# Latent attention in rounded parts, and the mixer's output projection divided along its inputs and run between the heads

## The chip, the cores and the metric

The kernel runs on one core of one Trainium2 chip. The time is device time of one launch in microseconds (us), as the median of several runs. A profile of one execution says when each instruction ran on each engine: TensorE (PE, and PEld for its weight loads), VectorE (DVE), ScalarE (ACT), GpSimd (POOL) and SyncE, whose queue (SPq) issues the DMAs.

## The reference, cut to what matters

Two transformer blocks over 256 latent tokens of width 1024. The second block has two layers and a second stream of 256 context tokens beside the latent one. Its first layer mixes tokens with a gated linear attention (GLA) and, beside it, with multi-head latent attention (four heads; 128 content and 64 rotary dimensions per key, 128 per value). Both outputs, 512 wide each, are joined, and one projection brings the 1024 inputs back to the model's width:

```python
def dense_attention(q, k, v, scale):
    s = jnp.einsum('bqhd,bkhd->bhqk', qi, k).astype(jnp.float32) * scale
    p = jax.nn.softmax(s, axis=-1).astype(v.dtype)
    return jnp.einsum('bhqk,bkhd->bqhd', p, v)
...
        yc, yl = even_mixer(hc, hl, cos, sin, even_w_in[i], ...)
        xl = post_norm(xl, g2 * yl)
        xl = post_norm(xl, 0.5 * g3 * swiglu(modulate(xl, sh3, sc3), ffn2_w_in[l], ffn2_w_out[l]))
        if not last:
            xc = post_norm(xc, cg2 * yc)
            xc = post_norm(xc, 0.5 * cg3 * swiglu(modulate(xc, csh3, csc3), ffn2_w_in[l], ffn2_w_out[l]))
```

Latent queries see all 512 keys (256 latent and 256 context), context queries the 256 context keys. All is float32.

## The kernel before

Activations lie with features on the 128 partitions and tokens along the free dimension: columns 0 to 255 are the latent stream, 256 to 511 the context. Dense products are made in rounded parts: every operand is held as a rounded high part and the remainder as a low part (type float32r), and `mm3` (line 221) makes high x high, high x low and low x high, three matmuls. `split` (line 256) makes the parts of an activation: a ScalarE copy that rounds, then a VectorE subtraction. `wunit` (line 198) does the same for a unit of weights of 128 x 1024 elements, 512 KB, behind its DMA; four staging tiles and three tiles each for high and low parts are shared by all weights of the kernel.

`even` (line 765) is the first layer's mixer. It projects, runs the GLA (`gla_core`, line 987), and then, from line 821, the part that the change touches:

- `mla` (line 917) for the context (`s=1`, two key tiles) and then for the latent stream (`s=0`, four key tiles). For each head and each of two query tiles, `weights` makes two full-precision score products (content, line 927, and rotary, line 928) into one PSUM bank `d` (four buffers), then row maximum, exponential, reciprocal and scaling (`softmax`, line 453); `finish` transposes the weights on TensorE (line 935), copies them out of PSUM (line 936), and after the second query tile `values` (line 942) makes the value products (line 945) and splits the head's output into `ym`. `push` (line 448) delays each `finish` by one step, so that the scores of one tile stand ahead of the transposes of the tile before.
- `gla_norm` (line 959) for both streams, between the two calls of `mla`, gives the linear attention's part `yg`.
- `mix_group` (line 744) is a quarter of the output projection for one stream: 256 output columns, eight input tiles (four from `yg`, four from `ym`), two weight units, 48 matmuls, and two gated additions into `res` (line 741). The context's four groups run one behind each latent head; the latent stream's four stand behind the heads.
- `after(1)` and `after(0)` are the layer norms (`post_ln`, line 342) and the modulation (line 368) of the context and of the latent stream, whose results `u` feed the next feed-forward products (`swiglu`, line 710), the context's first.

`need` (line 442) runs pieces of the conditioning's weight stream until its rows are there. Within an engine instructions run in order. That order is set at compile time by a scheduler that takes ready instructions by their place in the program, with offsets for weight splits (`AHEAD`) and for the emptying of PSUM (`EVAC`). Tile pools are stacked: the pool `mlaw` takes the memory of the GLA's closed pools, and an instruction that writes a tile waits for the last reader of what lay there.

Of the kernel before, what the change touches and what calls it, by code (L numbers as in the profile page):

```python
# [10 lines left out]
F32 = mybir.dt.float32  # L11
F32R = mybir.dt.float32r
# [6 lines left out]
P = 128  # L19
D = 1024  # L20
KD = D // P
S = 256
# [93 lines left out]
class Net:  # L116
# [28 lines left out]

    # ------------------------------------------------------------- set-up
    def setup(self):
# [48 lines left out]

    # ------------------------------------------------------------- dense pieces
    def wunit(self, w, k0, kc, c0, ncols):
# [60 lines left out]

    # ------------------------------------------------------------- token statistics  # L260
    def colsum(self, acc, n, T):
# [118 lines left out]

    # ------------------------------------------------------------- conditioning
    def ada_gen(self):
# [63 lines left out]

    # ------------------------------------------------------------- softmax attention pieces
    def push(self, step):
# [23 lines left out]

    # ------------------------------------------------------------- first block
    def bias_vec(self):
# [233 lines left out]

    # ------------------------------------------------------------- second block
    def swiglu(self, l, which, order, after, rate=0, orate=0):  # L710
# [54 lines left out]
    def even(self, after):  # L765
        nc, a = self.nc, self.a
        w = a["even_w_in_2"]
        u = self.u
        with ExitStack() as s0:
            go = self.pool(s0, "go", side="right")  # L770
            rg = self.t(go, [P, 4, 512], "rg")
            o = self.t(go, [P, 4, 512], "o")
            mo = self.pool(s0, "mo", side="right")
            qn = self.t(mo, [P, 4, 512], "qn")
            qr = self.t(mo, [P, 2, 512], "qr")
            kn = self.t(mo, [P, 4, 512], "kn")
            kr = self.t(mo, [P, 512], "kr")
            vl = self.t(mo, [P, 4, 512], "vl")
            with ExitStack() as s1:
# [6 lines left out]
                with ExitStack() as s2:  # L786
# [9 lines left out]
                    ps = self.feat(w, 8, 1536, (32, P), u, 0, 512)  # L796
# [4 lines left out]
                    ps = self.feat(w, 8, 1952, (P, 64), u, 0, 512)  # L801
# [22 lines left out]
            with ExitStack() as s2:  # L824
                mp = self.pool(s2, "mlaw")
                self.mla(mp, 1, ym, qn, qr, kn, kr, vl)
                self.gla_norm(1, o, rg, yg)
                self.gla_norm(0, o, rg, yg)
                x = yg[0] + ym[0], yg[1] + ym[1]
                self.need(0, 5)  # L830
                self.mla(mp, 0, ym, qn, qr, kn, kr, vl,
                         lambda g: self.mix_group(0, a["even_w_out_2"], x, 1, g))
            self.su = ExitStack()
            self.u = self.hilo(self.pool(self.su, "u2"), KD, 512, "u")
            after(1)
            for g in range(4):
                self.mix_group(0, a["even_w_out_2"], x, 0, g)
            after(0)
# [77 lines left out]

    def mla(self, mp, s, ym, qn, qr, kn, kr, vl, after=None):
        nc = self.nc
        k0, nk = (0, 4) if s == 0 else (2, 2)
        w = nk * P  # L920
        ks = slice(k0 * P, k0 * P + w)

        def weights(hd, it, pt):
            r = slice(64 * (hd % 2), 64 * (hd % 2) + 64)
            i0 = s * S + it * P
            ps = self.pd()
            nc.tensor.matmul(ps[:, :w], qn[:, hd, i0:i0 + P], kn[:, hd, ks], start=True, stop=False)  # L927
            nc.tensor.matmul(ps[:, :w], qr[r, hd // 2, i0:i0 + P], kr[r, ks], start=False, stop=True)  # L928
            scale = self.softmax(mp, ps, 1, w)

            def finish():
                p = scale()
                ptp = self.pm()
                for jt in range(nk):
                    nc.tensor.transpose(ptp[:, jt * P:(jt + 1) * P], p[:, 0, jt * P:(jt + 1) * P], self.ident)
                nc.vector.tensor_copy(pt[:, :nk, it * P:(it + 1) * P],
                                      ptp[:, :w].rearrange("p (j i) -> p j i", j=nk))
                if it == 1:
                    values(hd, pt)
            return finish  # L940

        def values(hd, pt):
            po = self.po()
            for jt in range(nk):
                nc.tensor.matmul(po[:, :S], vl[:, k0 + jt, hd * P:(hd + 1) * P], pt[:, jt, :],  # L945
                                 start=(jt == 0), stop=(jt == nk - 1))
            f = self.t(self.tmp, [P, S], "u", bufs=3)
            nc.vector.tensor_copy(f, po[:, :S])
            self.split(ym[0][hd][:, s * S:(s + 1) * S], ym[1][hd][:, s * S:(s + 1) * S], f)

        for hd in range(4):
            pt = self.t(mp, [P, 4, S], "pt", bufs=2)
            for it in range(2):
                self.push(weights(hd, it, pt))
            if after:
                after(hd)
        self.push(None)
# [148 lines left out]

    # ------------------------------------------------------------- head-split attention (64-wide heads, queries reversed)
    @urgent(EVAC)
# [52 lines left out]

    # ------------------------------------------------------------- neighbourhood layer
    def na_scratch(self):
# [160 lines left out]
```

## Time and profile before

| | us |
|---|---|
| median of 3 runs | 2373.38 |
| lowest and highest | 2372.59, 2376.87 |
| span of the profiled execution | 2370.2 |
| TensorE busy | 2280.1 |
| VectorE busy | 1740.7 |
| ScalarE busy | 1036.1 |
| GpSimd busy | 259.7 |

The span runs from the first to the last instruction of the profiled execution. Busy is the time in which an engine has at least one instruction in work; matmuls overlap, so the distance between the starts of two matmuls, not the duration of one, is what a matmul costs. A full-precision product appears as two matmul records. The granted clock is 1.00 at TensorE's higher level (2.4 GHz) and 0.50 at the lower (1.2 GHz).

### The profile page before, as it was taken

Reading aid. Unit: us, or ns where it says so; the run is one execution under the profiler, and the core shown is the slowest. Engines: PE = TensorE matmul, PEld = TensorE weight load, DVE = VectorE, ACT = ScalarE, POOL = GpSimd, SP = SyncE. Lnnn points to the kernel's source line nnn. Section 1 sums busy time; section 2 is a strip of 40 time slices with the busy share of each in tenths; the row PEclk is TensorE's granted clock in tenths of the full one; section 3 lists DMA queues with packets and bytes.
Section 4 is the critical chain, followed back from the end, with each engine's and each line's share of the span. In section 5 each row is a group of like instructions: output and inputs, shape, how many; then the busy total and the mean of one; then the engine's idle time right before and its main releaser. Section 6 shows DMA issues by size and latency. Waiting matters only on the chain.

```text
span 2370.2 us, 37198 instructions
## 1 busy us (share of the span) xinstructions
PE 2280.1 (96%) x14552; PEld 2037.5 (86%) x14552; DVE 1740.7 (73%) x2781; ACT 1036.1 (44%) x1710; POOL 259.7 (11%) x250
## 2 busy tenths in 40 slices
PE   8999999999999999889999999999999998998998
PEld 7999999998887987667898887998888898887998
DVE  7888887689998654675787777579788377776554
ACT  7765555532322434424442231353222256774442
POOL 1000000300000310340310000130000033101001
PEclk9999999999999999978999999999999999998998
DMA  8556566566666542111355555556555456524553
GB/s 250 167 157 192 170 198 209 182 204 204 189 203 191 165 123 75 44 63 37 116 177 178 168 162 153 172 159 202 176 171 173 134 174 170 145 71 123 183 179 110
DMA packets 336021, 374.22 MB, mean 158 GB/s; under 512 B 12531, under 2 KB 293781, under 8 KB 335846
## 3 DMA queue, kind: packets, MB, share of 16 engines
q1 hardware_dynamic: 335846, 371.85, 51.8%
q8 instruction: 114, 1.87, 0.3%
q14 instruction: 61, 0.50, 0.1%
HBM read 370.66 MB, written 1.14 MB: 157 GB/s over the span
## 4 chain that ended last, share of the span: by engine, by line
PE 57%; DVE 10%; DMA 5%; issue 3%; ACT 3%; POOL 1%; SPq 0%; DVEq 0%; POOLq 0%; ACTq 0%
PE d L224 17%; PE d L225 17%; PE d L226 17%; DMA st<-in_ada_w_dram 5%; DVE ada L403 3%; DVE lo L208 2%; ACT hi L207 1%; PE m L274 1%; PE d L928 1%; PE d L927 1%; DMA st<-drpb 1%; PE o L945 1%; PE o L1151 1%; POOL rr L286 0%; PE m L1197 0%
## 5 line engine op out<-in xcount | busy, mean ns | idle before, releaser
L224 PE MATMUL d<-uhi,hi 128*128 128x256 f32 (+1 forms) x2656 | 864.2, 327 | 6.0 <-ACT uhi L376 2.6
L208 DVE TENSOR_TENSOR lo<-st,hi 128x1024 fp32r<-128x1024 f32 (+1 forms) x548 | 657.4, 1201 | 286.2 <-ACT hi L207 283.7
L225 PE MATMUL d<-ulo,hi 128*128 128x256 f32 (+1 forms) x2656 | 864.4, 326 | 1.4 <-DVE ulo L379 1.4
L226 PE MATMUL d<-uhi,lo 128*128 128x256 f32 (+1 forms) x2656 | 863.4, 326 | 1.1 <-DVE lo L208 1.1
L207 ACT CAST hi<-st 128x1024 fp32r<-128x1024 f32 (+1 forms) x548 | 556.0, 1015 | 704.1 <-PE d L225 523.0
L224 PEld LDWEIGHTS d<-uhi,hi 128*128 128x128 f32 x2656 | 506.1, 191 | 51.5 <-ACT uhi L257 4.1
L225 PEld LDWEIGHTS d<-ulo,hi 128*128 128x128 f32 x2656 | 507.9, 191 | 42.7 <-DVE ulo L379 2.0
L226 PEld LDWEIGHTS d<-uhi,lo 128*128 128x128 f32 x2656 | 507.1, 191 | 43.0 <-DVE lo L208 1.5
L403 DVE SCALAR_TENSOR_TENSOR ada<-st,cs,ada 128x512 f32<-128x512 f32 x504 | 353.1, 746 | 113.1 <-DMA st<-in_ada_w_dram 113.0
L226 PE MATMUL d<-hhi,lo 128*128 128x256 f32 (+1 forms) x1144 | 353.8, 309 | 7.9 <-DVE lo L208 7.8
L224 PE MATMUL d<-hhi,hi 128*128 128x256 f32 (+1 forms) x1144 | 353.2, 309 | 0.0
L225 PE MATMUL d<-hlo,hi 128*128 128x256 f32 (+1 forms) x1144 | 352.6, 308 | 0.0
L226 PEld LDWEIGHTS d<-hhi,lo 128*128 128x128 f32 x1144 | 218.8, 191 | 21.3 <-DVE lo L208 10.8
L225 PEld LDWEIGHTS d<-hlo,hi 128*128 128x128 f32 x1144 | 218.9, 191 | 10.6
L224 PEld LDWEIGHTS d<-hhi,hi 128*128 128x128 f32 x1144 | 218.7, 191 | 10.3
L257 ACT CAST hhi<-hf 128x256 fp32r<-128x256 f32 (+1 forms) x122 | 60.6, 500 | 273.7 <-DVE hf L706 273.7
L348 POOL TENSOR_TENSOR acc<-res 128x256 f32<-128x256 f32 x10 | 11.1, 1110 | 1050.7 <-DVE res L741 1000.5
L224 PE MATMUL d<-hi,uhi 128*128 128x256 f32 x320 | 92.4, 290 | 8.7 <-DVE q L1117 6.4
L378 POOL TENSOR_SCALAR u<-res,sc,mods 128x256 f32<-128x256 f32 x88 | 78.1, 894 | 202.7 <-DVE sc L432 156.2
L225 PE MATMUL d<-lo,uhi 128*128 128x256 f32 x320 | 91.7, 288 | 0.0
L226 PE MATMUL d<-hi,ulo 128*128 128x256 f32 x320 | 91.0, 287 | 0.0
L725 ACT ACTIVATE sg<-d 128x512 f32<-128x512 f32 (+1 forms) x100 | 49.4, 494 | 55.4 <-PE d L226 55.3
(306 smaller groups left out, 2478.6 us busy)
## 6 DMA issues: line engine op xcount, KB each, us to landing
st<-in_ffn_w_in_dram SPq DMA_DIRECT2D x200, 512.0 KB, 3.8
st<-in_ada_w_dram SPq DMA_DIRECT2D x144, 512.0 KB, 3.8
st<-in_ffn_w_out_dram SPq DMA_DIRECT2D x110, 512.0 KB, 3.5
st<-in_na_w_in_dram SPq DMA_DIRECT2D x28, 512.0 KB, 4.2
st<-in_w_in_dram SPq DMA_DIRECT2D x24, 512.0 KB, 5.3
st<-in_w_gate_dram SPq DMA_DIRECT2D x22, 512.0 KB, 3.8
st<-in_w_up_dram SPq DMA_DIRECT2D x22, 512.0 KB, 4.4
st<-in_w_down_dram SPq DMA_DIRECT2D x20, 512.0 KB, 3.7
```

Source lines behind the costliest of these rows:

```text
L207: nc.scalar.copy(hi[:, :n], st[:, :n])
L208: nc.vector.tensor_sub(lo[:, :n], st[:, :n], hi[:, :n].bitcast(F32))
L224: nc.tensor.matmul(ps, lhi, rhi, start=first, stop=False)
L225: nc.tensor.matmul(ps, lhi, rlo, start=False, stop=False)
L226: nc.tensor.matmul(ps, llo, rhi, start=False, stop=last)
L257: self.nc.scalar.copy(hi, src)
L274: nc.tensor.matmul(ps[:, i * P:(i + 1) * P], col[:, i:i + 1].to_broadcast([P, P]), self.ident, start=True, stop=True)
L378: nc.gpsimd.tensor_scalar(u, z, sc, sh, op0=OP.mult, op1=OP.add)
L403: nc.vector.scalar_tensor_tensor(acc[:, s], st[:, i], c, acc[:, s], op0=OP.mult, op1=OP.add)
L725: nc.scalar.activation(s[:, :t1 - t0], ps[:, :t1 - t0], AF.Silu)
L927: nc.tensor.matmul(ps[:, :w], qn[:, hd, i0:i0 + P], kn[:, hd, ks], start=True, stop=False)
L928: nc.tensor.matmul(ps[:, :w], qr[r, hd // 2, i0:i0 + P], kr[r, ks], start=False, stop=True)
```

## The change

Queries, keys, values and softmax weights of the latent attention are split into high and low parts, and scores and values are made with `mm3`. For each head the parts lie in new tiles of the pool `mlaw` (two buffers for content queries, keys and values; one for the rotary parts; two and one for the transposed weights). The output projection is divided along its inputs: `mix_group` is called with input tiles 0 to 4 (`yg`) and 4 to 8 (`ym`) apart. The norms of the GLA and the context's first halves run between the context's heads; the context's second halves and the latent stream's first halves run behind the latent heads; the latent stream's second halves stay behind them. `need(0, 5)` stands ahead of the context's heads.

```diff
@@ even @@
-                self.mla(mp, 1, ym, qn, qr, kn, kr, vl)
-                self.gla_norm(1, o, rg, yg)
-                self.gla_norm(0, o, rg, yg)
+                heads = qn, qr, kn, kr, vl
                 x = yg[0] + ym[0], yg[1] + ym[1]
+                wo = a["even_w_out_2"]
                 self.need(0, 5)
-                self.mla(mp, 0, ym, qn, qr, kn, kr, vl,
-                         lambda g: self.mix_group(0, a["even_w_out_2"], x, 1, g))
+
+                def context(hd):
+                    if hd == 0:
+                        self.gla_norm(1, o, rg, yg)
+                    elif hd == 2:
+                        self.gla_norm(0, o, rg, yg)
+                    if hd:
+                        for g in ((0,), (1,), (2, 3))[hd - 1]:
+                            self.mix_group(0, wo, x, 1, g, 0, 4)
+
+                def latent(hd):
+                    self.mix_group(0, wo, x, 1, hd, 4, 8)
+                    self.mix_group(0, wo, x, 0, hd, 0, 4)
+
+                self.mla(mp, 1, ym, *heads, context)
+                self.mla(mp, 0, ym, *heads, latent)
             self.su = ExitStack()
             self.u = self.hilo(self.pool(self.su, "u2"), KD, 512, "u")
             after(1)
             for g in range(4):
-                self.mix_group(0, a["even_w_out_2"], x, 0, g)
+                self.mix_group(0, wo, x, 0, g, 4, 8)
             after(0)
@@ mla @@
+    def pair(self, pool, tag, bufs=2):
+        return [self.t(pool, [P, 512], tag + x, F32R, bufs=bufs) for x in "hl"]
+
+    def two(self, pool, shape, tag, src, bufs=1):
+        hi, lo = (self.t(pool, shape, tag + x, F32R, bufs=bufs) for x in "hl")
+        self.split(hi, lo, src)
+        return hi, lo
+
+        ts = slice(s * S, (s + 1) * S)
+        krs = [x[:, :w] for x in self.pair(mp, "kr", 1)]
+        self.split(*krs, kr[:, ks])
+        qrs = [None, None]
+
+        def head(hd):
+            if hd % 2 == 0:
+                qrs[0] = self.two(mp, [P, S], "qr", qr[:, hd // 2, ts])
+            q = self.two(mp, [P, S], "qn", qn[:, hd, ts], 2)
+            k = [x[:, :w] for x in self.pair(mp, "kn")]
+            self.split(*k, kn[:, hd, ks])
+            v = [x.rearrange("p (t i) -> p t i", t=4)[:, :nk] for x in self.pair(mp, "vl")]
+            self.split(*v, vl[:, k0:k0 + nk, hd * P:(hd + 1) * P])
+            return q, qrs[0], k, v
...
-            nc.tensor.matmul(ps[:, :w], qn[:, hd, i0:i0 + P], kn[:, hd, ks], start=True, stop=False)
-            nc.tensor.matmul(ps[:, :w], qr[r, hd // 2, i0:i0 + P], kr[r, ks], start=False, stop=True)
+            q, q2, k, v = parts
+            self.mm3(ps[:, :w], tuple(x[:, i] for x in q), k, True, False)
+            self.mm3(ps[:, :w], tuple(x[r, i] for x in q2), tuple(x[r] for x in krs), False, True)
...
-                nc.vector.tensor_copy(pt[:, :nk, it * P:(it + 1) * P],
-                                      ptp[:, :w].rearrange("p (j i) -> p j i", j=nk))
+                src = ptp[:, :w].rearrange("p (j i) -> p j i", j=nk)
+                h, l = (x[:, :nk, i] for x in pt)
+                nc.scalar.copy(h, src)
+                nc.vector.tensor_sub(l, src, h.bitcast(F32))
...
-                nc.tensor.matmul(po[:, :S], vl[:, k0 + jt, hd * P:(hd + 1) * P], pt[:, jt, :],
-                                 start=(jt == 0), stop=(jt == nk - 1))
+                self.mm3(po[:, :S], tuple(x[:, jt] for x in v), (pt[0][:, jt, :], pt[1][:, jt, :]), jt == 0, jt == nk - 1)
...
         for hd in range(4):
-            pt = self.t(mp, [P, 4, S], "pt", bufs=2)
+            parts = head(hd)
+            pt = [self.t(mp, [P, 4, S], "pt" + x, F32R, bufs=n) for x, n in (("h", 2), ("l", 1))]
             for it in range(2):
-                self.push(weights(hd, it, pt))
-            if after:
-                after(hd)
+                self.push(weights(hd, it, pt, parts))
+            after(hd)
```

## Rows read from the trace of the kernel before

**Rows 1.** Page, part 1: busy us (share of the span) and instructions.

```profile
PE 2280.1 (96%) x14552; PEld 2037.5 (86%) x14552; DVE 1740.7 (73%) x2781; ACT 1036.1 (44%) x1710; POOL 259.7 (11%) x250
```

**Rows 2.** Windows view: stretch, length, busy us (instructions) per engine, granted clock, DMA.

```profile
1000.00:1050.00 50.00, 41.99 (x332) 31.51 (x328) 44.37 (x70) 18.63 (x37) 30.70 (x25) 0.86 0.17 55
1050.87:1083.60 32.73, 32.66 (x95) 19.96 (x95) 10.33 (x28) 8.63 (x27) 2.49 (x2) 0.50 0.07 21
1070.65:1143.10 72.45, 71.53 (x392) 52.35 (x392) 43.79 (x98) 34.46 (x76) 7.16 (x7) 0.91 0.14 44
1143.10:1174.60 31.50, 28.25 (x217) 27.42 (x216) 24.00 (x45) 15.39 (x25) 15.19 (x15) 0.95 0.44 130
1174.60:1226.90 52.30, 48.54 (x396) 47.59 (x395) 40.35 (x66) 29.48 (x50) 12.46 (x13) 1.00 0.55 168
```

**Rows 3.** Timeline of TensorE, latent head 1: start, duration, line, output and inputs, count.

```profile
1118.63 1.02 PE L927 MATMUL d<-kn,qn 128*128 128x512 f32 x2
1119.58 1.12 PE L928 MATMUL d<-kr,qr 64*128 64x512 f32 x2
1120.63 0.66 PE L935 MATMUL m<-ident,p 128*128 128x128 f32 x4
...
1123.13 1.99 PE L945 MATMUL o<-pt,vl 128*128 128x256 f32 x8
1124.96 0.60 PE L935 MATMUL m<-ident,p 128*128 128x128 f32 x4
```

**Rows 4.** Timeline of TensorE: rounded products at full clock, then after a wait.

```profile
1126.10 0.28 PE L224 MATMUL d<-yghi,hi 128*128 128x256 f32 x1
1126.21 0.28 PE L225 MATMUL d<-yglo,hi 128*128 128x256 f32 x1
...
1270.04 0.39 PE L224 MATMUL d<-uhi,hi 128*128 128x512 f32 x1
1270.27 0.39 PE L225 MATMUL d<-ulo,hi 128*128 128x512 f32 x1
...
1160.80 0.41 PE L225 MATMUL d<-ymlo,hi 128*128 128x256 f32 x1
1161.01 0.41 PE L226 MATMUL d<-ymhi,lo 128*128 128x256 f32 x1
...
1162.69 0.28 PE L225 MATMUL d<-ymlo,hi 128*128 128x256 f32 x1
```

**Rows 5.** Timeline at the linear attention's end and in the context's heads.

```profile
1055.13 0.33 DVE L1060 SCALAR_TENSOR_TENSOR kv<-kv,dec 128x128 f32<-128x128 f32 x1
...
1057.77 1.22 PE L927 MATMUL d<-kn,qn 128*128 128x256 f32 x2
1058.92 1.12 PE L1068 MATMUL m<-vg,kd 128*64 128x128 f32 x8
...
1070.66 1.06 PE L928 MATMUL d<-kr,qr 64*128 64x256 f32 x2
...
1082.48 1.06 PE L927 MATMUL d<-kn,qn 128*128 128x256 f32 x2
```

**Rows 6.** Groups by line and form (min/median/max ns), then busy us and mean ns.

```profile
L258 DVE TENSOR_TENSOR hlo<-hf,hhi x122: 411/420/696, 277.4 to 2292.6; 128x256 fp32r<-128x256 f32 x68, 128x512 fp32r<-128x512 f32 x54
...
L257 ACT CAST hhi<-hf x122: 396/407/625, 276.3 to 2291.3; 128x256 fp32r<-128x256 f32 x68, 128x512 fp32r<-128x512 f32 x54
...
L208 DVE TENSOR_TENSOR lo<-st,hi 128x1024 fp32r<-128x1024 f32 x22 | 28.2, 1283 | 10.5 <-ACT hi L207 10.4
L741 DVE SCALAR_TENSOR_TENSOR res<-d,mods,res 128x256 f32<-128x256 f32 x16 | 7.7, 480 | 3.5 <-PE d L226 3.3
```

**Rows 7.** Timeline of SyncE's queue: the next conditioning load after the stretch.

```profile
1214.96 0.37 SPq L396 DMA_DIRECT2D st<-in_ada_w_dram  x1
```

**Rows 8.** Timeline of VectorE: the first and the eighth part of the context's u.

```profile
1163.89 0.41 DVE L379 TENSOR_TENSOR ulo<-u,uhi 128x256 fp32r<-128x256 f32 x1
...
1176.54 0.42 DVE L379 TENSOR_TENSOR ulo<-u,uhi 128x256 fp32r<-128x256 f32 x1 [0.38 <-POOL u L378]
```

More of the change, by code (lines that the diff above doesn't have):

```diff
@@ L915, in latent_proj, with mla @@
             self.rope_rot(rope, qf, qr[:, i, :])
-    def mla(self, mp, s, ym, qn, qr, kn, kr, vl, after=None):
+    def pair(self, pool, tag, bufs=2):
[4 more added lines that the diff above has]
+        return hi, lo
+    def mla(self, mp, s, ym, qn, qr, kn, kr, vl, after):
         nc = self.nc
@@ L921, in mla, with weights @@
         ks = slice(k0 * P, k0 * P + w)
-        def weights(hd, it, pt):
+        ts = slice(s * S, (s + 1) * S)
[11 more added lines that the diff above has]
+            return q, qrs[0], k, v
+        def weights(hd, it, pt, parts):
             r = slice(64 * (hd % 2), 64 * (hd % 2) + 64)
-            i0 = s * S + it * P
+            i = slice(it * P, it * P + P)
             ps = self.pd()
-            nc.tensor.matmul(ps[:, :w], qn[:, hd, i0:i0 + P], kn[:, hd, ks], start=True, stop=False)
-            nc.tensor.matmul(ps[:, :w], qr[r, hd // 2, i0:i0 + P], kr[r, ks], start=False, stop=True)
+            q, q2, k, v = parts
+            self.mm3(ps[:, :w], tuple(x[:, i] for x in q), k, True, False)
+            self.mm3(ps[:, :w], tuple(x[r, i] for x in q2), tuple(x[r] for x in krs), False, True)
             scale = self.softmax(mp, ps, 1, w)
@@ L935, in finish, with values @@
                     nc.tensor.transpose(ptp[:, jt * P:(jt + 1) * P], p[:, 0, jt * P:(jt + 1) * P], self.ident)
-                nc.vector.tensor_copy(pt[:, :nk, it * P:(it + 1) * P],
-                                      ptp[:, :w].rearrange("p (j i) -> p j i", j=nk))
+                src = ptp[:, :w].rearrange("p (j i) -> p j i", j=nk)
+                h, l = (x[:, :nk, i] for x in pt)
+                nc.scalar.copy(h, src)
+                nc.vector.tensor_sub(l, src, h.bitcast(F32))
                 if it == 1:
-                    values(hd, pt)
+                    values(hd, pt, v)
             return finish
-        def values(hd, pt):
+        def values(hd, pt, v):
             po = self.po()
             for jt in range(nk):
-                nc.tensor.matmul(po[:, :S], vl[:, k0 + jt, hd * P:(hd + 1) * P], pt[:, jt, :],
-                                 start=(jt == 0), stop=(jt == nk - 1))
+                self.mm3(po[:, :S], tuple(x[:, jt] for x in v), (pt[0][:, jt, :], pt[1][:, jt, :]), jt == 0, jt == nk - 1)
             f = self.t(self.tmp, [P, S], "u", bufs=3)
```

## Prediction

> **What bounds the kernel now.** I read the page's busy times first: TensorE is busy for 96% of a span of 2370.2 us [rows 1], so a change pays where it shortens TensorE's own work or a wait of TensorE. The code touched runs once, between the end of the gated linear attention and the first feed-forward product after it, so I then cut that stretch with the windows view [rows 2]. It shows five things. VectorE is the busy engine up to 1050 (44.37 of 50 us). From 1050.87 to 1083.6 TensorE is busy 32.66 of 32.73 us, yet its granted clock is 0.50, the lower level. From 1070.65 to 1143.1 (the heads, both norms of the linear attention, the context's output products) TensorE is busy 71.53 of 72.45 us, while VectorE is at 43.79 (60%) and ScalarE at 34.46. From 1143.1 to 1174.6 the latent stream's output products cover the context's layer norm, and TensorE is busy only 28.25 of 31.5 us. From 1174.6 to 1226.9 the context's first feed-forward products cover the latent stream's norm.
>
> The times are a median of 2373.4 us; the profiled execution has a span of 2370.2, 3.2 less, with what lies around it. I sum changes of the span and take them from the median. About 0.2%, 4.7 us, is what a measurement can tell from no change.
>
> **Products in rounded parts.** A full-precision product stands in the trace as two matmuls. Head 1 of the latent stream shows the prices at full clock [rows 3]: content scores 0.95 us (1118.63 to 1119.58), rotary scores 1.05, and four value products in 1.83, 0.46 each. A rounded product costs 0.11 us at 256 columns (0.114 over a run of them), 0.23 at 512, and at the low clock 0.21 at 256 [rows 4]; three of them cost 0.34, 0.68 and 0.64.
> - Latent scores, 16 calls: 8 x 0.27 + 8 x 0.37 = 5.1 us less. Latent values, 16 calls: 16 x 0.12 = 1.9 less.
> - Context values, 8 calls: 8 x 0.12 = 1.0 less; the first two run at the low clock, where a rounded call saves some 0.3 more: 1.6.
> - Context scores, 16 calls: seven run at 1.15 us before 1058.92, and are taken below; eight more, from 1070.66 to 1083.33 with other work between, took about 1.05 each at the low clock [rows 5], 8.4, and become 8 x 0.64 = 5.1; the last saves 0.3. Together 3.6 less.
>
> Sum: **-12.2 us**, all on TensorE, the engine that sets the end here.
>
> The seven early calls fill time in which TensorE would wait for VectorE: the recurrent state kv ends at 1055.46, and the linear attention's last products start behind the scores at 1058.92 and end at 1070.65, where the next score starts [rows 5]. The parts of head 0 lie in the pool `mlaw`, which takes the memory of the linear attention's pools. By the tile sizes (constants 11 KB, masks 4, then the query tile qi) the low part of the keys falls at 14 to 16 KB, on masks and qi, and qi is read until the end. Not ready early: the tail begins 3.5 us earlier, and 7 x 0.64 = 4.5 us of scores follow it, +1.0. Ready early: 7 x 0.51 = -3.6. I take **+1.0**.
>
> Clock: behind a wait of TensorE, rounded products start at the low clock (0.41 us long at 1160.80) and are at the high one by 1162.69 (0.28 long) [rows 4], while full-precision products stay at 0.50 up to 1083.6, 12.95 us behind 1070.65 [rows 2]. What is left of the context's heads would come back to the higher level some 6 us sooner, at half of each: **-3**, between 0 and -5.
>
> The Trainium skill (TensorE: Matmul & The Clock Gate, Part 1) says that activity releases the throttle; on that rule a stage without gaps comes back by itself, rounding adds nothing, and the sum below ends 3 us higher, a rival below. The trace doesn't agree that far: busy 32.66 of 32.73 us at 0.50 [rows 2].
>
> Rotary scores use 64 of 128 rows, and no row here has them rounded. The pair of full-precision matmuls costs 0.10 more than with 128 rows [rows 3], so a rounded one costs between nothing and 0.10 more; 16 calls x 3 gives 0 to 4.8. I take **+1.6**, as the pair's 0.05 each would give 2.4 and many loads hide.
>
> **What is added to VectorE and ScalarE.** The splits: context 15 of 256 columns (one shared rotary key, three for each of four heads, two rotary queries); latent 6 of 256 and 9 of 512. On VectorE a split costs 0.42 or 0.69 us, and on ScalarE 0.41 or 0.62 [rows 6] (median and longest of a group of both sizes). VectorE: 21 x 0.42 + 9 x 0.69 = 15.0. The transposed weights now leave PSUM by a ScalarE copy and a VectorE subtraction: the same on VectorE, and one more link, 0.41 or 0.62 us, ahead of the value products. Behind the waiting subtraction VectorE's queue holds the next row maxima and the low parts of the output weight, for which the softmax and the half products wait; TensorE's cover for the link is the next score, 0.68 to 1.36 us, and without it 16 passes would cost some 8 us. Half products double the gated additions; up to the context's last one there are 24 where 8 were, 16 x 0.48 = 7.7 us. Of the output weight's units of 512 KB the count stays 16, but four more are split before that point: 4 x 1.28 = 5.1 [rows 6]. So VectorE goes from 43.8 to about 71.5 us of busy time, and ScalarE from 34.5 to about 61 (14.2 of splits, 8.2 of copies, 4.2 of casts).
>
> TensorE's own length of that stretch becomes 72.45 - 11.7 (the last head's values lie behind it) + 4.5 (the early scores) - 3 + 1.6 + 8.4 (three latent half products, 24 x 0.117 each, moved in) = 72.2. VectorE and TensorE would be level. If the splits hide wholly, the cost is 0; if VectorE reaches the 89% that it has in 1000 to 1050 [rows 2], the stretch lasts 71.5 / 0.887 = 80.6, +8.4. I take **+6**, nearer to the row, as some splits fall into the empty time ahead of 1067.
>
> **What is moved.** The conditioning's `need(0, 5)` moves ahead of the heads, past SyncE's queue. The queue issues no conditioning load until 1214.96 [rows 7], so it emits nothing: 0. If it did, each load of 512 KB would stand ahead of the output weight on SyncE.
>
> The cover of the context's norm shrinks. Behind the context's last product (1143.1) TensorE had 192 x 0.118 + 2.4 = 25.1 us of work in 31.5, losing 6.4. After, it has 24 products, the last head's end and 96 products: 16.6 us. The norm gives its first part of u at 1163.89 + 0.4, 21.2 us behind 1143.1, and the eighth at 1176.96, 33.9 behind [rows 8]. With a chunk each 1.0 us the eighth comes at 28.2 and the first two units, 5.7 us of work, end at 30; TensorE loses 30 - 5.7 - 16.6 = 7.7, and 1.5 at the low clock after its wait: +2.8. Fewer weight splits lie in the norm's way: I take **+2**. Ends: -2 (chunks at 0.85 and an earlier first), and +8.5 (the eighth at 33.9 as now).
>
> The latent norm then starts while TensorE still waits for the context's, some 6 us earlier against its cover. Now 384 x 0.12 = 46.1 us of products take 52.3 [rows 2]: 6.2 lost. I take **-2**, between -4 and 0.
>
> Sum: -12.2 + 1.0 - 3 + 1.6 + 6 + 2 - 2 = **-6.6**: 2366.8 us, a span of 2363.6.
>
> **Rivals.**
> - *TensorE stays the bound.* The splits run ahead in the idle time of both engines (ScalarE has 38 us free, [rows 2]) and cost nothing: -6.6 - 6 = -12.6, 2360.8. For it: double buffers of keys, queries and values. Against it: VectorE's 71.5 us.
> - *Half of it is lost.* Either the clock stays low as long as now, as the skill's rule would leave it: -3.6, 2369.8; or the context's norm comes as late as now, +6.5: 2373.3. Against the first: products at the low clock between 1160.4 and 1162.5.
> - *VectorE becomes the bound of the heads, and it is slower.* Place: the stretch that now is 1070.65 to 1143.1. VectorE runs in order, each split waits for ScalarE's cast, and scores wait for the split. At a share of 80% the stretch lasts 71.5 / 0.8 = 89.4, 17.2 more than TensorE's own, and the kernel is 4.6 us slower, 2378; at 78% (91.7) it is at 2380. It decides from a share of 84%, where the cost is 12.6 and the gain is gone.
> - *The change doesn't do what it says:* the scheduler puts the half products behind the heads. Then the context's norm is later by their work and the cover is again full; with the splits as forecast about 2370.
>
> **How the numbers follow.** Forecast (-4.7 to -9) 0.34; TensorE the bound 0.21; half lost, or half products not moved, 0.25, within 0.2%; VectorE the bound 0.20. Faster 0.55, same 0.25, slower 0.20. The range takes in the first rival with early scores (2360.8 - 4.6, about 2356) and VectorE at 78% (2380).
>
> **What would show it.** Right: scores of three matmuls at 0.68 us a call; VectorE at 85 to 95% between the linear attention's end and the context's last product; the clock back at 1.0 within some 5 us of the first rounded scores; a wait of 5 to 10 us on TensorE for the context's u. Wrong: context scores before the linear attention's last products; VectorE under 80% while TensorE waits for splits; a head of the latent stream that takes longer than the 12.2 us of now.

## The result and the profile after

The changed kernel takes 2388.55 us against 2373.6: 1.0056 times the kernel before, with a 95% interval of 1.0040 to 1.0071. Run again on two other chips beside the kernel before it gave 1.0043 (1.0025 to 1.0060) and 1.0059 (1.0045 to 1.0073). It is slower by 10 to 14 us where 6.6 less were forecast. Its profiled execution has a span of 2386.0. Page, part 1, beside [rows 1]:

```profile
PE 2285.1 (96%) x14608; PEld 2049.0 (86%) x14608; DVE 1758.4 (74%) x2827; ACT 1052.6 (44%) x1756; POOL 260.3 (11%) x250
```

TensorE is busy 5.0 us more, not less. To find where, I compare the starts of the same matmul in each trace. A is the 1,153rd matmul of the form d<-uhi,hi (867.89 us in the trace of before), ahead of all that was changed; B the 1,322nd (1200.87, "the unit at 1200" below), in the feed-forward layer behind the mixer; C the last, the 2,656th (2289.84). From B on, both kernels have the same instructions. The scheduler placed them in another order up to about 1215 us on TensorE and 1272 on VectorE (trace of before). From the 1,463rd matmul of that form (1275.48) on, the order too is the same on TensorE, VectorE, ScalarE and GpSimd.

| us | A to B | B to C |
|---|---|---|
| before, three executions | 333.0, 335.1, 334.9 | 1089.0, 1093.1, 1089.5 |
| after, three executions | 340.3, 339.3, 337.8 | 1101.2, 1099.4, 1102.0 |

So there are two losses: 5 us in the stage that the change touches, and 10 us behind it, where nothing was edited. The second isn't a matter of order: from the 1,463rd matmul to C the same three executions took 1014.4, 1018.7 and 1015.0 us before, 1026.1, 1024.3 and 1026.8 after.

The stage first. Windows of after, beside [rows 2] (stretch, length, then busy us and instructions of PE, PEld, DVE, ACT, POOL, granted clock, DMA). The linear attention's last product ends at 1063.93, the context's last output product at 1155.85, and the context's feed-forward products begin at 1178.92:

```profile
1046.86:1051.00 4.14, 0.00 (x2) 0.03 (x1) 3.30 (x6) 0.00 (x0) 2.49 (x2) 0.50 0.64 212
1051.00:1063.93 12.93, 12.89 (x48) 9.18 (x48) 1.42 (x3) 1.49 (x4) 0.00 (x0) 0.50 0.00 0
1065.60:1073.30 7.70, 7.69 (x25) 5.85 (x26) 3.60 (x12) 3.89 (x13) 0.00 (x0) 0.50 0.00 0
1063.93:1083.00 19.07, 15.40 (x62) 13.48 (x61) 8.26 (x26) 9.71 (x30) 1.65 (x1) 0.50 0.00 1
1083.00:1096.50 13.50, 13.50 (x101) 12.20 (x99) 10.19 (x29) 8.56 (x23) 0.00 (x0) 0.99 0.12 41
1096.50:1104.00 7.50, 7.50 (x37) 7.13 (x36) 3.41 (x9) 3.11 (x9) 1.64 (x1) 0.54 0.22 70
1120.00:1140.00 20.00, 19.93 (x133) 16.16 (x132) 18.36 (x34) 13.93 (x25) 3.84 (x3) 1.00 0.30 101
1063.93:1155.85 91.92, 86.48 (x531) 74.35 (x531) 66.11 (x149) 54.43 (x125) 8.65 (x7) 0.86 0.18 58
1155.85:1178.92 23.07, 19.43 (x148) 17.73 (x148) 20.35 (x37) 10.35 (x18) 9.21 (x10) 0.93 0.45 134
1178.92:1231.20 52.28, 50.29 (x393) 49.19 (x394) 41.12 (x71) 32.03 (x54) 16.34 (x18) 0.97 0.45 140
```

Four things are to be seen. TensorE does nothing for 4.14 us at 1046.86, where before it made context scores [rows 5]. From 1063.93 to 1083 the clock is 0.50, and it falls to it again from 1097.0 to 1103.9. VectorE's share up to 1155.85 is 72% (66.11 of 91.92), not 85 to 95%. And TensorE is busy 86.48 of these 91.92 us. What it waited for there (waits view of after, 1064 to 1156: line, releaser, us in total, times, longest):

```profile
PE m L274 <- POOL rr L286: 2.0, 1, 2.0
PE d L224 <- ACT knh L257: 1.7, 1, 1.7
PE o L225 <- DVE ptl L976: 1.5, 1, 1.5
```

Only 1.5 us in the heads are a wait for VectorE. Nearly all else is TensorE's own work. Its time from each matmul's start to the next one's, by kind, from the end of the linear attention's last product to B (first profile of each):

| us | before | after |
|---|---|---|
| context scores | 8.78 | 11.91 |
| latent scores | 15.45 | 14.35 |
| context, latent values | 4.98, 7.03 | 3.58, 6.40 |
| norms' column sums and spreads | 9.31 | 14.29 |
| layer norms' means | 0.56 | 1.59 |
| transposes | 6.64 | 5.07 |
| output products | 48.03 | 49.62 |
| feed-forward products | 21.31 | 22.86 |
| idle (after: 1.68 of it ahead of the first score) | 7.92 | 10.88 |

Outside the table, the linear attention ends 3.2 us sooner, counted from A (199.77 for 202.97), as its last products no longer stand behind scores. The columns add up to 130.0 and 140.6 us, so 10.5 more and 3.2 less make the 7.3 us of this pair of profiles. In the two other profiles of after the norms' sums and spreads took 13.1 and 13.0 us; between executions of one kernel the feed-forward and output products differ by up to 1.5 us, the idle time by up to 0.6, the other rows by up to 0.2. TensorE's first feed-forward and last layer-norm products ran at 0.50 in after (1175.5 to 1182.4), where in before that spell lay at 1159.2 to 1162.6.

### The profile page after: what moved, and what is told of

The parts are those of the page before. It is cut to its first block, busy times and chain, and to the rows that moved or that the text cites. A ratio compares the mean times of both kernels' runs of the same rounds, so it can differ in the third digit from the quotient of the medians.

```text
span 2386.0 us, 37398 instructions
## 1 busy us (share of the span) xinstructions
PE 2285.1 (96%) x14608; PEld 2049.0 (86%) x14608; DVE 1758.4 (74%) x2827; ACT 1052.6 (44%) x1756; POOL 260.3 (11%) x250
## 4 chain that ended last, share of the span: by engine, by line
PE 53%; DVE 13%; DMA 7%; issue 4%; ACT 3%; POOL 2%; DVEq 0%; SPq 0%; POOLq 0%; ACTq 0%
PE d L224 16%; PE d L225 16%; PE d L226 16%; DMA st<-in_ada_w_dram 6%; DVE ada L403 3%; DVE lo L208 3%; ACT hi L207 1%; PE m L274 1%; DVE adt L409 1%; DVE hf L706 1%; PE o L1189 1%; DMA st<-drpb 1%; DVE hlo L258 0%; PE m L1235 0%; DVE adr L410 0%
## 5 line engine op out<-in xcount | busy, mean ns | idle before, releaser
L224 PEld LDWEIGHTS d<-hhi,hi 128*128 128x128 f32 x1144 | 218.7, 191 | 10.3
```

The source lines that it names most:

```text
L224: nc.tensor.matmul(ps, lhi, rhi, start=first, stop=False)
```

## The experiments

Theory A: TensorE lost. Its filler inside the linear attention is gone, and more of its work falls to the lower clock. Theory B: the new order (norms between the heads, doubled additions) is at fault. Theory C: VectorE's splits take what the products give. Theories F, N and R came up on the way, and each stands where it did.

**Two controls.** The kernels before and after, unchanged, each profiled again.

> The kernel before, unchanged, profiled a second time. Expected 2373.6 us within 0.1%. Its use: the two profiles lay 3.7 us apart already at the 865th us, ahead of the change, and behind the mixer the distance grew from some 1 us to 15.8 us although the instructions there are the same. If such drifts are chance of one execution, the two profiles of the kernel before lie apart by several us too, here and there; if they follow from the change, the two lie within 2 us everywhere.

Measured: 0.9998 (0.9980 to 1.0016). B to C took 1093.1 us for 1089.0 in the first profile, so 4 us there come without any edit. Runs of one kernel on this chip went from 2371 to 2387 us. Single times therefore say little: the ratios and the two distances are what I compare.

> The changed kernel, unchanged, a second time. Expected 1.0056 of the kernel before (2387). Stretch from the end of the linear attention's last product to the first feed-forward product of the context: 115.0 us as in its first profile, where the kernel before takes 103.7. If the loss lies in the stage alone, the feed-forward products that cover the latent norm start 1 to 5 us later than in the kernel before and the end keeps that distance; if there is a loss of its own further down, the distance grows again by 8 to 12 us between there and the end.

Measured: 1.0043. The stretch up to the context's first feed-forward product took 113.2 us, not 115.0; A to B 339.3; B to C 1099.4. The second loss is there again.

**The two halves of the change alone.** `order_alone` has the new `even` and the old `mla`; `parts_alone` the old `even` and the new `mla`.

> The divided projection and its new order alone; the attention's products stay full-precision as before. Theory A (the parts cost TensorE its filler: context scores that ran in the wait for VectorE inside the linear attention come behind it, and they and the norm's products run at the lower clock): scores again ahead of 1060 us, stage no more than 2 us longer than in the kernel before (103.7), time 2368 to 2376. Theory B (the order itself costs: norms of the linear attention between the context's heads, at the low clock, and twice the gated additions): stage 6 to 10 us longer, 2380 to 2387.

Measured: 1.0003 (0.9989 to 1.0017), A to B 335.2. Scores stood inside the linear attention again. Theory B falls: the order costs some 1 us in the stage. B to C took 1095.9.

> The rounded parts alone; the norms and the projection stay whole and where they were. Theory A: the context scores come behind the linear attention, TensorE waits some 4 us there with nothing to fill it, and the gain of the rounded products (some 10 us) is offset by it and by the low clock: 2372 to 2380. Theory B: the parts themselves pay, 2362 to 2367. VectorE as the bound would show as waits of TensorE for low parts of 5 us and more in the heads.

Measured: 1.0018 (1.0003 to 1.0033), A to B 342.0, B to C 1097.6. The profiled execution was the longest of this kernel (2390.8 us, median 2384.2), so these distances are at the upper end. All 48 context scores came behind the linear attention. The loss in the stage comes with the parts, as A says. On this chip B to C took 1093.1 us before, 1095.9 with the order alone, 1097.6 with the parts alone and 1099.4 with both. In the timed runs the two halves add up to 0.0021, the whole change to 0.0043 or more: some of the loss may belong to neither half alone, which intervals of 0.003 leave open.

**Why the scores came late.** ScalarE's timeline of after at the linear attention's end (start, duration, line, operation, in brackets the idle time before it and what ended it):

```profile
1057.32 0.37 ACT L1108 COPY kv<-m 128x256 f32<-128x256 f32 x1 [0.24 <-PE m L1106]
1062.10 0.37 ACT L1128 COPY o<-o 128x256 f32<-128x256 f32 x1 [4.41 <-PE o L1127]
1063.97 0.37 ACT L1128 COPY o<-m 128x256 f32<-128x256 f32 x1 [1.50 <-PE m L1127]
1064.24 0.41 ACT L257 CAST krh<-kr 128x256 fp32r<-128x256 f32 x1
```

ScalarE is idle, yet the first part is made right behind the last copy of the linear attention. `early_parts` puts the parts of context heads 0 and 1 into a small pool opened ahead of the linear attention's, and into tiles of the pool `tmp`:

```diff
+                    self.own = self.pool(sm, "own")
...
+            if early and hd == 0:
+                q, k = mine(self.tmp, "acc", 3), mine(self.own, "kn", 1)
```

> The changed kernel with the rounded parts of the context's heads 0 and 1 in memory that the linear attention doesn't use (other tiles of the pool are reused to make room, and the softmax tile has two buffers for three). Theory A: the scores of head 0 at least run in the 4 us wait of TensorE inside the linear attention, the wait behind its last product goes, and first mark to the unit at 1200 takes 333 to 337 us against 339 to 340 in the changed kernel. If the scores were late for another reason than memory, they stay behind the linear attention's last product and nothing changes.

Measured: A to B 333.4 us. The wait was filled. TensorE's timeline of `early_parts`:

```profile
1053.18 0.79 PE L1147 MATMUL m<-qi,kv 64*128 64x128 f32 x2
1053.90 0.58 PE L225 MATMUL d<-knh,acc 128*128 128x256 f32 x1
...
1057.31 0.41 PE L227 MATMUL d<-krh,qrl 64*128 64x256 f32 x1
1057.88 1.12 PE L1126 MATMUL m<-vg,kd 128*64 128x128 f32 x8 [0.16 <-DVE kd L1113]
```

Both query tiles of head 0, twelve products, stand where TensorE sat idle. The stage is as short as before; memory was the reason, and it cost 6 us. The kernel is still at 1.0035 (1.0023 to 1.0047), as B to C takes 1098.5.

**What the latent heads gain.** Here the context's heads are in full precision, the latent ones in parts.

> Rounded parts for the latent heads alone, the context's heads in full precision as before, with the new order of the projection. Theory A (TensorE's lost filler and the lower clock cost the gain): context scores fill the wait inside the linear attention again, the clock comes back by 1080 as in the kernel with the order alone, the latent heads keep their 7 us; first mark to the unit at 1200 takes 327 to 331 us against 333 to 335 before. Theory C (VectorE's splits in the latent heads cost what the products gain): 334 to 337 us.

Measured: 1.0021 (1.0006 to 1.0037), A to B 335.4. My theory A failed here: filler and clock were back (at 1.0 from 13.2 us behind the linear attention, as in before, but for 3.4 us at 1094), and still nothing was gained over `order_alone` (335.2). B to C took 1097.7. The latent scores took 14.43 us for 16.05 there, not 11, and what they gave went into the norms' sums and spreads, 14.2 for 12.5, some of them in that spell. No wait for VectorE explains the scores; the timelines of TensorE and of its weight loads do (after, one query tile, beside [rows 3]):

```profile
1135.00 0.39 PE L224 MATMUL d<-knh,qnh 128*128 128x512 f32 x1
1135.23 0.40 PE L225 MATMUL d<-knl,qnh 128*128 128x512 f32 x1
1135.46 0.40 PE L226 MATMUL d<-knh,qnl 128*128 128x512 f32 x1
1135.79 0.50 PE L224 MATMUL d<-krh,qrh 64*128 64x512 f32 x1
1136.13 0.39 PE L225 MATMUL d<-krl,qrh 64*128 64x512 f32 x1
1136.36 0.39 PE L226 MATMUL d<-krh,qrl 64*128 64x512 f32 x1
1136.68 0.65 PE L972 MATMUL m<-ident,p 128*128 128x128 f32 x4
```

```profile
1135.00 0.19 PEld L225 LDWEIGHTS d<-knl,qnh 128*128 128x128 f32 x1
1135.23 0.19 PEld L226 LDWEIGHTS d<-knh,qnl 128*128 128x128 f32 x1
1135.79 0.18 PEld L224 LDWEIGHTS d<-krh,qrh 64*128 64x128 f32 x1 [0.37 <-issue]
1135.90 0.19 PEld L225 LDWEIGHTS d<-krl,qrh 64*128 64x128 f32 x1
1136.13 0.18 PEld L226 LDWEIGHTS d<-krh,qrl 64*128 64x128 f32 x1
1136.68 0.42 PEld L972 LDWEIGHTS m<-ident,p 128*128 128x128 f32 x4 [0.36 <-issue]
```

Between products of 128 rows the next weights are loaded while the matmul before runs, and starts are 0.23 us apart. The load of the 64-row tile (1135.79) starts only 0.33 behind the last 128-row product, the second rotary product starts 0.34 behind the first, and the first 128-row tile behind the rotary products (1136.68) is as late, 0.32. This query tile pays 0.1 us three times. The Trainium skill (TensorE: Matmul & The Clock Gate, Part 3, The mechanism) has loads pulled ahead of matmuls in flight if their row group doesn't conflict or they go to the background weight buffer. The trace agrees between tiles of 128 rows, 0.23 apart, and not at a change of height.

Theory R takes this as the price. The keys' tile holds the same 64 rows twice, so a query tile whose other half is set to zero once gives the same scores with 128 rows:

```diff
+            self.split(*(x[r] for x in qrs[hd % 2]), qr[r, hd // 2, ts])
...
-            self.mm3(ps[:, :w], tuple(x[r, i] for x in q2), tuple(x[r] for x in krs), False, True)
+            self.mm3(ps[:, :w], tuple(x[:, i] for x in q2), krs, False, True)
```

> The changed kernel with the rotary queries of each head in 128 rows, the other head's 64 rows zero, against all 128 rows of the keys (which hold the same 64 twice); the softmax tile has two buffers for three. Theory R: in the changed kernel a weight tile of 64 rows isn't loaded beside a product of 128 rows, nor the other way, so that the latent scores cost 14.4 us instead of 11 and save 1.1 us against before instead of 3.5. With full rows they take 10.9 to 11.5 us, the context's 10.2 to 10.8 instead of 11.9, and first mark to the unit at 1200 takes 334 to 337 us instead of 340. If the price comes from elsewhere (late low parts from VectorE, weight loads as such), the latent scores stay at 14 us.

Measured: 1.0010 (1.0001 to 1.0019), A to B 332.8. One query tile of `full_rows`:

```profile
1124.45 0.40 PE L225 MATMUL d<-knh,qnh 128*128 128x512 f32 x1
1124.69 0.40 PE L226 MATMUL d<-knl,qnh 128*128 128x512 f32 x1
1124.92 0.39 PE L227 MATMUL d<-knh,qnl 128*128 128x512 f32 x1
1125.15 0.39 PE L225 MATMUL d<-krh,qr0h 128*128 128x512 f32 x1
1125.38 0.39 PE L226 MATMUL d<-krl,qr0h 128*128 128x512 f32 x1
```

The starts here are 0.23 apart throughout: R holds. The latent scores took 12.7 us, the context's 8.3 for 11.9: 5.2 of the 7 us gained. Eight of the 48 latent products, from 1105.31 to 1108.28, ran at a granted clock of 0.53 and took 3.4 us; the other 40 took 9.3, 0.23 each, so without that spell they would be near the 11 of R. Part of the context's share is the clock, which in this execution was at 1.0 from 1067.1 to 1070.5. B to C took 1091.1.

> The kernel before, its order unchanged, with the latent heads alone in rounded parts and their rotary queries in 128 rows; the context's heads stay in full precision, and the norms and the output projection stay where they were. By theories A and R this keeps the filler and the clock and pays: latent scores 11 us for 15.4, values 6.4 for 7.0, first mark to the unit at 1200 in 328 to 331 us for 333 to 335, time 3 to 6 us below the kernel before unless the stretch behind the mixer gives it back. If VectorE's splits are the price, 334 us and more.

Measured: 0.9994 (0.9984 to 1.0003), A to B 332.0, latent scores 12.1 us, B to C 1082.4. A second time, on another chip:

> Latent heads alone in rounded parts with 128 rows, order as before, a second time (0.9994 in the first). Stage 332 us, 3 better than before, behind the mixer 1082 to 1090 us: 0.9980 to 0.9995. If the first was chance on the good side, 1.000.

Measured: 0.9995 (0.9980 to 1.0010), A to B 332.9, B to C 1095.3. The gain of 2 to 3 us in the stage is there, that of the whole can't be told from nothing. The same kernel differs by 13 us behind the mixer between the two chips, so that distance is compared on one chip only. Up to B TensorE's idle time behind the linear attention is 10.3 us in it, where the kernel before has 7.5 to 8.1; the scores give 3.0 (24.2 to 21.2), so most of that goes into waits.

**Both remedies together.**

> The changed kernel with both remedies: context heads 0 and 1 in memory of their own, rotary queries in 128 rows (to make room the softmax tile has two buffers for three and the high part of the transposed weights one for two). Each alone brought the stage from 340 to 333 us. If they add, first mark to the unit at 1200 takes 327 to 330 us, against 333 to 335 before, and the kernel is 4 to 6 us faster than before (0.9975 to 0.9985) if nothing is lost behind; if they overlap, 331 to 333 us and a ratio of 0.999 to 1.0005.

Measured: A to B 329.9, 8 us less than the changed kernel and 5 less than before on this chip. They add, though not in full: alone they gave 6 and 7. The ratio is 1.0011 (0.9997 to 1.0025) all the same, since B to C took 1103.4.

**The loss behind the mixer.** The waits of TensorE for weights from 1230 us on, in before and after on one chip (`before_third`, `after_third`):

```profile
PE d L226 <- DVE lo L208: 5.9, 3, 5.1
```

```profile
PE d L226 <- DVE lo L208: 13.1, 10, 4.2
```

The weights come late, though their loads are issued in the same order. Of the 12.6 us that the stretch is longer, 7.2 are this wait; the rest is spread over many short distances, and no run here explains it. The page lists a second kind of DMA, "instruction": 115 packets of 16 KB on queue 8 in after, 114 in before, for 29,423 and 29,314 instructions of TensorE: one for 256. Theory F says that such a piece delays a weight load beside it, and that the change, by 112 instructions more, moves all later pieces. The Trainium skill (Runtime: NRT & Kernel Launch, Instruction fetch mechanics) also has blocks of 16 KB or 256 instructions on a queue of their own, and calls their cost mostly hidden. Theory N: it is chance.

> The kernel before with 28 tiny full-precision matmuls added to the warm-up at its start, where TensorE waits for its first data; they are 112 instructions of TensorE, as many as the change adds in the mixer. Nothing else differs. Theory F: the DMA engines also bring TensorE's instructions, in pieces of 16 KB for every 256 instructions, and a piece makes a weight load beside it land some 1.3 us late; the change shifts these pieces by 112 instructions, onto loads that TensorE waits for. Then the mixer stage stays (333 to 335 us from the first ffn1 mark to the unit at 1200), and from there to the last feed-forward product it takes 1096 to 1101 us instead of 1089 to 1093; time 4 to 8 us above the kernel before. Theory N (what the changed kernel loses behind the mixer is chance, or is handed on by the later stage): within 2 us of the kernel before.

> The changed kernel with 36 tiny matmuls in the warm-up, 144 instructions, so that with the 112 of the change the pieces of the instruction stream stand behind the mixer where they stand in the kernel before. Theory F: the stretch behind the mixer takes 1089 to 1094 us instead of 1100, the mixer stage stays at 339 to 341, time 5 to 8 us below the changed kernel, some 1.002 of the kernel before. Theory N: no difference from the changed kernel, 1.005.

Both are inconclusive. The small matmuls weren't free: the first real product came at 23.6 and 27.1 us instead of 12.5 to 14.6, as the warm-up had already filled that wait. Ratios 1.0061 and 1.0080; B to C 1096.3, as F has it, and 1097.9, as F doesn't. The next two replace warm-up products instead, and start near the old time (13.9 and 15.3 us). The edit of `before_shift`; `after_shift` has 38 for 30:

```diff
-WARM = 5
+WARM = 3
...
+        for _ in range(30):
+            nc.tensor.matmul(warm[:1, :1], self.onesm[:, :1], self.onesm[:, :1], start=True, stop=True)
```

> The kernel before with two of its five warm-up products replaced by 30 very small ones (one weight column, one column): 112 instructions of TensorE more, at the start, which should cost no time there. Theory F (pieces of the instruction stream, moved onto weight loads that TensorE waits for, are what the changed kernel loses behind the mixer): the stretch from the unit at 1200 to the last feed-forward product takes 1096 to 1101 us instead of 1089 to 1093, and the time is 4 to 8 us above the kernel before (1.0017 to 1.0034). Theory N: 0.999 to 1.001.

Measured: 1.0002 (0.9991 to 1.0014), B to C 1086.3: F missed.

> The changed kernel with two warm-up products replaced by 38 very small ones: 144 instructions more, so that behind the mixer the pieces of the instruction stream stand as in the kernel before. Theory F: 1089 to 1094 us behind the mixer instead of 1100, time 5 to 8 us below the changed kernel (1.001 to 1.003 of the kernel before). Theory N: as the changed kernel, 1.004 to 1.006.

Measured: 1.0032 (1.0020 to 1.0045), A to B 339.2, B to C 1086.1. This is short of F's distance, and the ratio lies between the two forecasts; but it was another chip, on which the kernel before took 2364.9. On the same chip `full_rows`, without a shift, took 1091.1. So all three went onto one chip:

> The kernel before, unchanged, for its profile on the same chip as the three kernels beside it. First mark to the unit at 1200: 333 to 335 us. Behind it: 1085 to 1093 us, by the chip.

> The changed kernel, unchanged. First mark to the unit at 1200: 339 to 340 us, 5 to 6 more than the kernel before. If the loss behind the mixer belongs to the change, the stretch behind it takes 6 to 10 us more than in before_third and the ratio is 1.0045 to 1.0055; if it was the chip or chance, the stretch is within 3 us of before_third and the ratio 1.002 to 1.0035.

> The changed kernel with 144 small instructions ahead, a second time. If the place of the instruction stream's pieces matters, its ratio is at least 0.0015 below that of after_third on the same chip; if not, the two agree within 0.001.

Measured: B to C 1089.5 before, 1102.0 after, 1092.9 after with the shift. The loss belongs to the change (12.6 us here), and with 144 small instructions at the start of the program 9 of it are gone. In the timed runs the shift is worth less: 1.0059 (1.0045 to 1.0073) against 1.0042 (1.0025 to 1.0058), intervals that overlap; its first real product comes 2.0 us later (15.6 for 13.7). One place shows how. DMA view of three loads of 512 KB, 39 to 30.5 us ahead of the 2,042nd matmul d<-uhi,hi; `after_third`, then `after_shift_again`, then `before_third` (queue: packets, MB, share; then issues with the median us from issue to landing):

```profile
q8 instruction: 1, 0.02, 1.7%
issues: line engine op xcount, KB each, median us to landing
st<-in_ffn_w_in_dram SPq DMA_DIRECT2D x3, 512.0 KB, 5.1
```

```profile
q14 instruction: 1, 0.01, 0.2%
issues: line engine op xcount, KB each, median us to landing
st<-in_ffn_w_in_dram SPq DMA_DIRECT2D x3, 512.0 KB, 3.6
```

```profile
issues: line engine op xcount, KB each, median us to landing
st<-in_ffn_w_in_dram SPq DMA_DIRECT2D x3, 512.0 KB, 3.7
```

The median is that of the two loads whose landing shows. With a piece of 16 KB beside it, a load lands 1.4 us later, and TensorE, which there lives from load to load, waits. The first two profiles of after have the same piece there and landings of 4.6 to 5.8 us. The distance over the two stretches from the 1,701st to the 2,042nd and on to the 2,101st was 376.9 us in `after_third`, 371.5 in `after_shift_again` and 371.6 in `before_third`: here the shift gives back all of 5.3 us. Only the first stretch holds the place shown: 206.3, 204.3 and 204.2 us, of which 1.9 is one longer distance, ahead of a product with a weight's low part (1785.7 in `after_third`). In the second (170.6, 167.3 and 167.4) the load at fault isn't shown.

Elsewhere a piece does the same, but less. Behind B the traces have the landing of 203 loads of 512 KB. The 53 that meet a piece only in `after_third` land 0.36 us later there (standard error 0.08) than in `after_shift_again`; the 57 that meet one only in `after_shift_again` land 0.20 (0.07) later there; the 93 that meet none differ by 0.03. Both kernels have 54 or 55 pieces behind B: the change moves them, and which load each one meets decides.

> early_rows with 144 small instructions of TensorE ahead. If the place of the instruction stream's pieces is what early_rows (stage 330 us, 5 better than before, yet 1.0011) loses behind the mixer, the two stretches that end at the marks 1773 and 1941 take 204 and 167 us as in the kernel before (206.9 and 171.5 in early_rows), the stretch behind the mixer 1088 to 1095 us instead of 1103, and the ratio falls to 0.997 to 0.9995. If the loss has another source, the stretch stays at 1100 us and the ratio at 1.001.

Measured: 0.9997 (0.9980 to 1.0014), A to B 330.0, B to C 1098.1; the two stretches 206.3 and 169.0. B to C is 5.3 us less than without the shift, though on another chip; 3.2 of it lie in these two, and they still take 375.3, not 371.6. With both remedies and the shift, the kernel is level with before, not faster.

Settled: the loss behind the mixer is the change's, 6 to 13 us between profiles of one chip, and more than half of it is waits for late weights. Shown: pieces of the instruction stream make loads late, by 1.4 us at one place, which cost TensorE 1.9 us, and by 0.2 to 0.4 on average. Open: how much of the 6 to 13 us the pieces make, and why the kernel before didn't suffer from a shift (the piece at the three loads lay 3 us later there than in after, and the load beside it landed in 4.3 us).

## Why the prediction was wrong

- **Latent scores: mis-sized.** -5.1 was the term, and half of the +1.6, which covers the rotary products of both streams; measured 15.45 to 14.35, that is -1.1. Against 48 products at 0.227 the extra of the latent scores alone was 3.5, more than the 2.4 that half of the bound 0 to 4.8 allows: the bound gave 0.10 to each rotary product, but the first 128-row product behind them pays too. The choice leaned on "many loads hide", and exactly these don't. The pair of full-precision products also cost 0.5 less in sum than head 1's row said.
- **Values: mis-sized.** -1.9 and -1.6; measured -0.6 and -1.4. A run of products at 0.114 [rows 4] is not a group of twelve that other work cuts into: the latent ones cost 0.40 a call, not 0.34.
- **Context scores and the early ones: right in direction, too small.** That head 0's parts can't be ready was read correctly, and `early_parts` shows the reason. The tail began 3.2 us sooner (3.5 forecast), but the scores behind it took 3.1 us more than before instead of 0.9 (4.5 late scores less 3.6), and the wait for their first part 1.7 more.
- **Clock: wrong sign, the step that failed most.** -3 was forecast from rounded products that had sped up at 1160 to 1162 [rows 4]. In after, 7.69 of 7.70 us of rounded scores from 1065.60 left the clock at 0.50. The linear attention's first norm then ran at the lower clock (1073.7 to 1083), and the spreads of the second too (1101.6 to 1104.6), where before all of both ran at 1.00 behind the context's heads: +5.0 for column sums and spreads (+3.7 to +3.8 in the other two profiles of after, where the clock didn't fall again). I moved the norm in the sum as if its price moved along. The clock came back at about 1083, 19 us behind the linear attention, and 20 and 21 in the other two; before it took 13 [rows 2]. The rule of the Trainium skill (TensorE: Matmul & The Clock Gate, Part 1) that activity releases the throttle gets no support from these stretches, busy as they were.
- **VectorE: didn't become the bound.** +6 was forecast; TensorE waited 1.5 us for it in the heads and 1.7 for ScalarE at their start. VectorE did reach 18.36 of 20 us between 1120 and 1140, yet its parts were early enough (that the double buffers did it is not shown). The rival "VectorE becomes the bound" had the right sign and the wrong mechanism.
- **Norms: the waits nearly right, the gain not.** Behind the context's last product TensorE lost 3.6 us (23.07 less 19.43) against 3.3 before: +0.4 for +2. The latent norm's wait went from 3.8 to 2.0, -1.8 for -2, but its stretch took 52.28 us for 52.30: the products began it at the lower clock (up to 1182.4; 0.97 on the mean for 1.00) and took what the wait gave.
- **Behind the mixer: not in the sum at all.** Work whose order doesn't change was counted as unchanged. It took 10 us more, the larger part of the miss: a term put at nothing without a reason.

The stage came out 5 us longer, within the bounds of the unknown costs; with the 10 us behind it the time left the range.

## What to carry over

Price a moved or rounded step by the neighbours that it will have: the same matmul cost 0.23 us beside tiles of its own height and 0.33 at a change of height, and the same norms 9.3 or 13.0 to 14.3 us by the clock of their place. Work that fills another engine's wait is worth its whole length, and new tiles in reused memory can take it out of that wait though the edit names no such move. Before a difference is put down to an edit, compare the stretch behind it, where nothing was edited: here it held the larger part.

## What the runs showed of the hardware

- A weight load of 64 rows was not made beside a product of 128 rows, nor the reverse: 0.33 us between starts for 0.23 (after, 1135.46 and 1136.36).
- There was one 16 KB piece of the instruction stream on queue 8 for every 256 TensorE instructions (115 for 29,423). Loads of 512 KB around one took 5.1 us to land instead of 3.6 at the place shown; over 53 loads a piece cost 0.36 us on average.
- The granted clock stayed at 0.50 through 12.89 busy us of 12.93, then 7.69 of 7.70; and it fell again at 1097.0, though TensorE had been busy 13.50 of the 13.50 us up to 1096.5. Twelve column sums of one column each (1093.57 to 1094.83) were among that work; in the two other profiles of after, which have them too, the clock didn't fall there.
